# Down product of an MLP: first contributions copied by ScalarE, residual added two tiles a step later

## Chip, core and metric

One Trainium2 chip, one of its cores. The metric is the device time of one execution in microseconds (us); three executions were timed and their median is given.

## What is computed

The kernel is one layer of a streaming encoder: a mixer (gated short convolution beside a state-space scan), an output projection with a residual, then an MLP with a residual and a last normalisation. This case is about the MLP's second product:

```python
x = x + jnp.einsum("btc,cd->btd", y, w_out)                       # x1 below
h = rmsnorm(x, norm_mlp_w)
hid = jnp.square(jax.nn.relu(jnp.einsum("btd,df->btf", h, w_up)))
return x + jnp.einsum("btf,fd->btd", hid, w_down)                 # this sum, 2048 tokens x 1024
```

followed by `rmsnorm(x, final_norm_w)`. Everything is float32; 2048 tokens, width 1024, hidden width 4096.

## The kernel before

**Arithmetic.** Each operand is split into a high and a low part (`hi`, `lo`), and a product is three matmuls: hi·hi, hi·lo, lo·hi (lines 296 to 298). Matrices are multiplied in blocks of 2 x 2 by a seven-product scheme. `chain` (L265) issues the seven products of a step in the order b11, t1, t2, b21, t3, b22, t4. They run in three PSUM accumulators, called `x`, `y` and `w` (tiles `px`, `py`, `pw`): b11, t2, t3 and t4 add one after the other into `x`, t1 and b22 into `y`, b21 into `w`. ScalarE copies `x` into `w` after b11 (L303, the seed), so that b21 adds on top of b11. A product that goes on in an accumulator may start only when the value before it has been read: t3 needs the reading after t2, t4 that after t3, b22 that after t1.

**Down product.** `down` (L1036) walks `STEPS`. A step takes four hidden blocks (places) for one output block `d` of a token half `h`; near the start and the middle a step holds one or two shorter groups: step 0 is (h 0, d 0, four places), step 1 (0, 2, two places), step 2 the two groups (0, 1, one place) and (0, 3, three places), and from step 3 on four places each, with h 1 coming in at step 15. A place is 128 channels deep, so a product over four places is 12 matmuls. For each (h, d) four accumulators of 128 x 512 float32 lie in SBUF: `c11`, `c22`, `c12`, `c21` (tiles `acc`). They are made by `outs` (L1019), which at once loads the residual `x1_d` into them (L1026). `evict` (L1055) then adds each PSUM value to its accumulator on VectorE (L1069): t1 to c22, t2 to c12, b21 to c11, then t3 to c22, b22 to c12, t4 to c21. The reading after b11 is left out when the seed was made.

**Where accumulators lie.** The pool tag `utmp` has 8 tiles of 512 columns, `uhid` 5 of 2 x 512. `two` (L1029) hands them out in units; the 16 accumulators of the first half take all 8 `utmp` and four `uhid`. The fifth `uhid` is the first unit of the second half (unit 8).

**Feeding.** Weights of the next step are loaded by SyncE (`wraw`, L999), cast by ScalarE (`whi`, L100) and their low part made by VectorE (`wlo`, L101; sums of blocks L252 and L229). Hidden blocks come back from DRAM by SyncE (`rh`, L1016), are cast by ScalarE (`uh`, L368) and get their low part from VectorE (`ul`, L369). The last pair of the up product runs just before step 0, with its own evictions (L912, L915, L918, L919) and its stores (`hid_d`, L902 and L903).

**Order.** A scheduler places the instructions on each engine from the program's dependences; each engine then works through its list in that order. So the edit moves instructions beyond the lines that it touches.

Of the kernel before, what the change touches and what calls it, by code (L numbers as in the profile page):

```python
# [14 lines left out]
ALU = mybir.AluOpType  # L15
# [15 lines left out]
NBB = TH // TB  # L31
# [9 lines left out]
def trunk(ctx: ExitStack, tc: tile.TileContext, x, w_in, w_dt, w_out, w_up, w_down, cvec, hrow, out):  # L41
    nc = tc.nc
# [15 lines left out]
    x1_d = spill("x1", NB)  # L58
# [21 lines left out]
        out=tri, in_=tri, compare_op=ALU.is_ge, fill=0.0, base=0, pattern=[[1, P]], channel_multiplier=-1  # L80
# [789 lines left out]
    class Mlp(Seven):  # L870
# [148 lines left out]
        def outs(self, h, d):  # L1019

            t = {}
            self.units = 2 * d if h == 0 else max(self.units, 8)
            for two in ((("c11", 0, 0), ("c22", 4, 1)), (("c12", 0, 1), ("c21", 4, 0))):
                for a, (n, i, bb) in zip(self.two(), two):
                    t[n] = a
                    nc.sync.dma_start(a, x1_d[h * NBB + bb][:, d + i])  # L1026
            self.acc[h, d] = t

        def two(self):  # L1029
            n, self.units = self.units % 9, self.units + 1  # L1030
            if n < 4:
                return [self.tmp("acc") for _ in range(2)]
            t = self.wide("acc")
            return [t[:, i] for i in range(2)]

        def down(self, ws):  # L1036
            late = None
            for n, step in enumerate(STEPS):
                last = n + 1 == len(STEPS)
                ahead = self.rest_weights() if last else self.weights(self.load_down(STEPS[n + 1]))  # L1040
                groups = [[self.wides[h * NQ + f] for f in fs] for h, d, fs in step]
                if not last:
                    for h, d, fs in STEPS[n + 1]:
                        if (h, d) not in self.acc:
                            self.outs(h, d)
                if n == N_FIRST + 3:
                    late = self.finish_first()

                def done(name, gi):
                    h, d, fs = step[gi]  # L1050
                    if h == 0 and fs[-1] == NQ - 1:
                        i, bb = {"c11": (0, 0), "c22": (4, 1), "c12": (0, 1), "c21": (4, 0)}[name]
                        nc.sync.dma_start(fin_d[d + i][:, bb * TB : (bb + 1) * TB], self.acc[h, d][name])

                def evict(name, gi, pm):  # L1055
                    h, d, fs = step[gi]
                    c, p, fin = {
                        "b11": ("c11", "x", 0),
                        "t1": ("c22", "y", 0),
                        "t2": ("c12", "x", 0),  # L1060
                        "b21": ("c11", "w", 1),
                        "t3": ("c22", "x", 1),
                        "b22": ("c12", "y", 1),
                        "t4": ("c21", "x", 1),
                    }[name]
                    t = self.acc[h, d][c]
                    if name == "b11" and gi in self.seeds:
                        return
                    nc.vector.tensor_tensor(out=t, in0=pm[p], in1=t, op=ALU.add)  # L1069
                    if fin:  # L1070
                        done(c, gi)

                def after(name):
                    if late is not None and name in ("b11", "t2", "t3"):
                        next(late, None)
                    g = REFILL.get(n)
                    if g is not None:
                        self.refill((g,), name)
                    if last and name == "t4":
                        self.rest_blocks()  # L1080

                ws = self.chain(groups, ws, ahead, evict, after)
            for _ in late:
                pass
            self.rest(ws)
# [131 lines left out]
    for n in range(1, 2 * NQ - 3):  # L1217
        fs = list(range(n, n + 4))
        step = [(h, n % 4, [f % NQ for f in fs if f // NQ == h]) for h in range(2)]
# [228 lines left out]
    class Output:  # L1448
# [62 lines left out]
        def residual(self, n):  # L1511
            if n < len(self.UNITS):
                i, b, d = self.UNITS[n]
                t = self.xt[n] = self.xp.tile([P, TB], F32, tag="xt", name="xt", bufs=3)
                nc.sync.dma_start(t, x[b, :, d] if i == 0 else x1_d[b][:, d])
# [185 lines left out]
```

## Time and profile before

| | us |
|---|---|
| median of three executions | 2631.99 |
| lowest, highest | 2627.35, 2633.1 |
| the profiled execution's own time | 2631.43 |
| its span in the trace | 2629.4 |

The span leaves out 2.0 us of the profiled execution's own time. Matmul rows overlap: a row lasts 0.39 us, while the next one starts 0.23 us after it. A bracket such as [0.68 <-DVE acc L1069] at a row's end is the time for which the engine stood idle before it and what released it. A row "us in total, times, longest" belongs to the view of waits. In the view of windows each engine's busy time is followed by the count of its instructions; then come the granted TensorE clock, the share of the DMA engines and GB/s.

### The profile page before, as it was taken

The numbers are of one execution on the slowest core, as the hardware profiler recorded it, in microseconds if no ns is written. First come the engines' busy times: TensorE is split into PE (matmuls) and PEld (weight loads), VectorE is DVE, ScalarE is ACT, GpSimd is POOL, SyncE is SP. The second block draws the span as 40 slices with busy tenths as digits, with TensorE's granted clock in tenths as the row PEclk, the third lists the DMA queues.
The fourth block names the chain that finished last, engine by engine and source line by source line (L and its number), as shares of the span: only waits on it lengthen the run. The fifth ranks groups of instructions, "written<-read, shape, count | busy, mean of one in ns | idle before, by whom it ended". The sixth has DMA issues, their size and how long they took to land.

```text
span 2629.4 us, 33773 instructions
## 1 busy us (share of the span) xinstructions
PE 2599.6 (99%) x12139; PEld 2139.1 (81%) x12139; DVE 1917.2 (73%) x2631; ACT 1458.9 (55%) x2213; POOL 59.0 (2%) x99
## 2 busy tenths in 40 slices
PE   9999999999999999999999999999999999999998
PEld 7788888788888888878888888888887788888887
DVE  7877877777777767778677775744448877888985
ACT  7554345776667666768335555755555444444443
POOL 1010000000000000000000000000000000000001
PEclk9999999999999999999999999999999999999999
DMA  4545735555555578877656786765558544665762
GB/s 156 192 174 184 280 142 193 181 179 162 171 168 169 165 266 262 266 223 232 206 196 236 263 320 232 280 213 194 190 195 299 154 149 154 212 209 168 251 206 77
DMA packets 252167, 536.96 MB, mean 204 GB/s; under 512 B 26208, under 2 KB 93024, under 8 KB 252000
## 3 DMA queue, kind: packets, MB, share of 16 engines
q1 hardware_dynamic: 251856, 534.29, 60.7%
q8 instruction: 95, 1.56, 0.2%
q14 instruction: 72, 0.59, 0.1%
q10 hardware_dynamic: 144, 0.52, 0.1%
HBM read 354.89 MB, written 179.83 MB: 203 GB/s over the span
## 4 chain that ended last, share of the span: by engine, by line
PE 66%; issue 24%; DMA 4%; ACT 3%; DVE 2%; POOL 0%; SPq 0%; POOLq 0%; DVEq 0%; ACTq 0%
PE px L296 9%; PE px L298 9%; PE px L297 9%; PE py L296 5%; PE py L298 5%; PE py L297 5%; PE pm L113 4%; PE pm L114 4%; PE pm L115 4%; PE pw L296 2%; PE pw L298 2%; PE pw L297 2%; PE yd L1350 1%; PE yo L1347 1%; DMA dec<-rd_d 1%
## 5 line engine op out<-in xcount | busy, mean ns | idle before, releaser
L296 PE MATMUL px<-uh,whi 128*128 128x512 f32 x1672 | 656.1, 392 | 8.3 <-DVE acc L1069 5.6
L298 PE MATMUL px<-uh,wlo 128*128 128x512 f32 x1672 | 651.0, 390 | 0.0
L297 PE MATMUL px<-ul,whi 128*128 128x512 f32 x1672 | 651.0, 389 | 0.0
L296 PEld LDWEIGHTS px<-uh,whi 128*128 128x128 f32 x1672 | 313.8, 188 | 82.0 <-DVE acc L1069 4.8
L101 DVE TENSOR_TENSOR wlo<-wraw,whi 128x512 fp32r<-128x512 f32 (+1 forms) x213 | 221.4, 1039 | 212.2 <-ACT whi L100 212.1
L298 PEld LDWEIGHTS px<-uh,wlo 128*128 128x128 f32 x1672 | 313.9, 188 | 66.1 <-issue 0.2
L100 ACT CAST whi<-wraw 128x1024 fp32r<-128x1024 f32 x214 | 193.9, 906 | 310.3 <-PE px L297 217.4
L297 PEld LDWEIGHTS px<-ul,whi 128*128 128x128 f32 x1672 | 314.0, 188 | 63.6
L100 ACT CAST whi<-s 128x1024 fp32r<-128x1024 f32 x210 | 219.7, 1047 | 221.3 <-PE py L297 87.4
L296 PE MATMUL py<-uh,whi 128*128 128x512 f32 x836 | 327.3, 392 | 2.5 <-ACT eb L802 1.2
L297 PE MATMUL py<-ul,whi 128*128 128x512 f32 x836 | 325.8, 390 | 0.0
L298 PE MATMUL py<-uh,wlo 128*128 128x512 f32 x836 | 325.4, 389 | 0.0
L101 DVE TENSOR_TENSOR wlo<-s,whi 128x1024 fp32r<-128x1024 f32 x210 | 255.3, 1216 | 68.7 <-ACT whi L100 65.9
L113 PE MATMUL pm<-uh,whi 128*128 128x512 f32 (+1 forms) x648 | 251.2, 388 | 0.1
L114 PE MATMUL pm<-ul,whi 128*128 128x512 f32 (+1 forms) x648 | 247.8, 382 | 0.5 <-DVE ul L226 0.5
L115 PE MATMUL pm<-uh,wlo 128*128 128x512 f32 (+1 forms) x648 | 247.9, 383 | 0.0
L296 PEld LDWEIGHTS py<-uh,whi 128*128 128x128 f32 x836 | 156.9, 188 | 38.0 <-ACT eb L802 1.6
L298 PEld LDWEIGHTS py<-uh,wlo 128*128 128x128 f32 x836 | 157.0, 188 | 32.7
L297 PEld LDWEIGHTS py<-ul,whi 128*128 128x128 f32 x836 | 157.0, 188 | 32.1
L368 ACT CAST uh<-rh 128x1024 fp32r<-128x1024 f32 (+1 forms) x128 | 120.3, 944 | 83.0 <-PE py L298 65.7
L296 PE MATMUL pw<-uh,whi 128*128 128x512 f32 x418 | 163.3, 391 | 0.0
L298 PE MATMUL pw<-uh,wlo 128*128 128x512 f32 x418 | 162.8, 389 | 0.0
(245 smaller groups left out, 3786.6 us busy)
## 6 DMA issues: line engine op xcount, KB each, us to landing
hid_d<-e SPq DMA_DIRECT2D x96, 512.0 KB, 3.8
rh<-hid_d SPq DMA_DIRECT2D x96, 512.0 KB, 4.2
wraw<-w_in SPq DMA_DIRECT2D x68, 512.0 KB, 3.7
wraw<-w_down SPq DMA_DIRECT2D x104, 256.0 KB, 3.6
wraw<-w_up SPq DMA_DIRECT2D x48, 512.0 KB, 4.2
dec<-rd_d SPq DMA_DIRECT2D x32, 512.0 KB, 5.5
wraw<-w_out SPq DMA_DIRECT2D x32, 512.0 KB, 5.2
x_d<-xt SPq DMA_DIRECT2D x64, 256.0 KB, 3.7
```

The costliest lines, as they stand in the source:

```text
L100: nc.scalar.copy(hi, raw)
L101: eng.tensor_tensor(out=lo, in0=raw, in1=hi.bitcast(F32), op=ALU.subtract)
L113: nc.tensor.matmul(out, whi, hi, start=(k == 0), stop=False)
L114: nc.tensor.matmul(out, whi, lo, start=False, stop=False)
L115: nc.tensor.matmul(out, wlo, hi, start=False, stop=(k == nk - 1))
L296: nc.tensor.matmul(p, hi, h[0], start=not seeded and k == 0, stop=False, **kw)
L297: nc.tensor.matmul(p, hi, h[1], start=False, stop=False, **kw)
L298: nc.tensor.matmul(p, lo, h[0], start=False, stop=(k == len(g) - 1), **kw)
L368: nc.scalar.copy(p[i][0], t)
L1347: nc.tensor.matmul(yo[:, j * L : (j + 1) * L], state[:, j * P : (j + 1) * P], cT, start=True, stop=True)
L1350: nc.tensor.matmul(yd[(i % 2) * 64 : (i % 2) * 64 + 64, (i // 2) * L : (i // 2 + 1) * L], byhead(t["xdt"])[:, i, :], t["dec"][:, i % 2 * 4 ...
```

## The change

`outs` makes the accumulators of the first token half (h 0) without loading anything into them. For a step whose (h 0, d) has not been met before, the first value for each accumulator is copied there by ScalarE (`nc.scalar.copy`, L1096 after) in place of VectorE's add: after t1 (c22), t2 (c12), b21 (c11) and t4 (c21). That is four copies for each of four output blocks d, 16 in all, in steps 0, 1 and 2. The residual follows in steps 3 to 10: the new generator `residual` loads two tiles a step into one spare `uhid` tile (`res`) and adds them to their accumulators on VectorE (L1043 after), 16 loads and 16 adds. The spare tile is then handed out as unit 8, as the fifth `uhid` tile was before. The second half (h 1) is as before. The changed kernel's lines from 1024 on stand up to 30 lines further down: L1069 is L1098 there.

```diff
-            for two in ((("c11", 0, 0), ("c22", 4, 1)), (("c12", 0, 1), ("c21", 4, 0))):
+            for two in self.TWOS:
                 for a, (n, i, bb) in zip(self.two(), two):
                     t[n] = a
-                    nc.sync.dma_start(a, x1_d[h * NBB + bb][:, d + i])
+                    if h:
+                        nc.sync.dma_start(a, x1_d[h * NBB + bb][:, d + i])
             self.acc[h, d] = t
+
+        TWOS = ((("c11", 0, 0), ("c22", 4, 1)), (("c12", 0, 1), ("c21", 4, 0)))
+
+        def residual(self, m):
+
+            if self.spare is None:
+                self.spare = self.wide("res")
+            d = (m + 3) % 4
+            for j, (n, i, bb) in enumerate(self.TWOS[m // 4]):
+                nc.sync.dma_start(self.spare[:, j], x1_d[bb][:, d + i])
+            yield
+            yield
+            for j, (n, i, bb) in enumerate(self.TWOS[m // 4]):
+                t = self.acc[0, d][n]
+                nc.vector.tensor_tensor(out=t, in0=t, in1=self.spare[:, j], op=ALU.add)
+                yield
...
-            t = self.wide("acc")
+            if n == 8 and self.spare is not None:
+                t, self.spare = self.spare, None
+            else:
+                t = self.wide("acc")
...
+                left = self.residual(n - 3) if 3 <= n < 11 else iter(())
+                fresh = [h == 0 and (h, d) not in begun for h, d, _ in step]
+                begun.update((h, d) for h, d, _ in step)
...
-                    nc.vector.tensor_tensor(out=t, in0=pm[p], in1=t, op=ALU.add)
+                    if fresh[gi] and (name in ("b11", "t1", "t2", "t4") or (name == "b21" and gi in self.seeds)):
+                        nc.scalar.copy(t, pm[p])
+                    else:
+                        nc.vector.tensor_tensor(out=t, in0=pm[p], in1=t, op=ALU.add)
...
                 def after(name):
+                    next(left, None)
```

What this does to the lists of the engines, at three places. First SyncE, between the last reloads of hidden blocks for step 0 (`rh`) and the weights of step 1 (`wraw`, 128 x 256) and step 2 (`wraw`, 128 x 128 and 128 x 384); `x_d` is the residual. Before:

```order
L1016 DMA rh<-hid_d_3_116 128x512
L1026 DMA acc<-x_d_77 128x512
L902 DMA hid_d_15_144<-e_16756 128x1024
L902 DMA hid_d_15_144<-e_16757 128x1024
L1026 DMA acc<-x_d_78 128x512
L903 DMA hid_d_15_144<-t_16755 128x512
L1026 DMA acc<-x_d_78 128x512
L1026 DMA acc<-x_d_77 128x512
L999 DMA wraw<-w_down 128x256 x4
L1026 DMA acc<-x_d_77 128x512
```

And now, from the reloads of the third kind (128 x 1024) on:

```order
L999 DMA wraw<-w_down 128x256 x2
L1016 DMA rh<-hid_d_1_114 128x1024
L1016 DMA rh<-hid_d_2_115 128x1024
L1016 DMA rh<-hid_d_3_116 128x1024
L999 DMA wraw<-w_down 128x256 x2
L1016 DMA rh<-hid_d_0_113 128x512
L899 DMA b_d<-e_16756 128x512
L1016 DMA rh<-hid_d_1_114 128x512
L902 DMA hid_d_15_144<-e_16758 128x1024
L1016 DMA rh<-hid_d_2_115 128x512
L1016 DMA rh<-hid_d_3_116 128x512
L999 DMA wraw<-w_down 128x128 x2
```

The residual's loads are gone from here, and the weights of step 1 are issued ahead of seven (their first half) and of four (their second) of the reloads, where they stood behind all of them.

Second ScalarE, at the end of the same reloads (casts `uh`) and in step 1. Before:

```order
L368 CAST uh_16975<-rh 128x512
L368 CAST uh_16979<-rh 128x512
L368 CAST uh_16983<-rh 128x512
L368 CAST uh_16987<-rh 128x512
L100 CAST whi<-wraw 128x512
L100 CAST whi<-s_17071 128x512
L303 COPY pw<-px 128x512
```

Now:

```order
L368 CAST uh_16975<-rh 128x512
L100 CAST whi<-wraw 128x512
L368 CAST uh_16979<-rh 128x512
L368 CAST uh_16983<-rh 128x512
L1096 COPY acc<-py 128x512
L1096 COPY acc<-px 128x512
L1096 COPY acc<-pw 128x512
L303 COPY pw<-px 128x512
L100 CAST whi<-s_17063 128x512
L100 CAST whi<-s_17096 128x512
L100 CAST whi<-wraw 128x256
L1096 COPY acc<-px 128x512
```

The cast of step 1's first weights moved between the reloads' casts, and step 0's copies after t1, t2 and b21 stand behind the last of those casts.

Third VectorE, where the first residual adds (`res`) stand, at the turn from step 2 to step 3; two `px` adds are the readings after t3 of step 2's two groups, the `py` adds those after b22. Now:

```order
L101 TENSOR_TENSOR wlo<-s_17290,whi 128x1024
L1098 TENSOR_TENSOR acc<-px,acc 128x512 x2
L1098 TENSOR_TENSOR acc<-py,acc 128x512
L1043 TENSOR_TENSOR acc<-acc,res 128x512
L252 TENSOR_TENSOR s_17443<-wraw 128x512
L1098 TENSOR_TENSOR acc<-py,acc 128x512
L369 TENSOR_TENSOR ul_17339<-rh,uh_17338 128x1024
L101 TENSOR_TENSOR wlo<-s_17331,whi 128x1024
```

And in each of the last four of the eight steps, ahead of the readings after t1 (`py`) and t2 (`px`):

```order
L229 TENSOR_TENSOR s_17933<-wraw,s_17893 128x512
L1043 TENSOR_TENSOR acc<-acc,res 128x512 x2
L369 TENSOR_TENSOR ul_17857<-rh,uh_17856 128x1024
L1098 TENSOR_TENSOR acc<-py,acc 128x512
L1098 TENSOR_TENSOR acc<-px,acc 128x512
```

The first add stands behind step 2's readings after t3, and the later pairs behind a step's last reading and ahead of the next step's first.

TensorE's list changes too: the first product of step 1 (b11, six matmuls) moved from behind step 0's t4 to the place between step 0's b21 and b22.

```order
L298 MATMUL pw_17011<-uh1_16880,wlo_16858 128x512
L296 MATMUL px_17126<-uh0_16802,whi_17059 128x512
L297 MATMUL px_17126<-ul0_16803,whi_17059 128x512
L298 MATMUL px_17126<-uh0_16802,wlo_17060 128x512
L296 MATMUL px_17126<-uh0_16806,whi_17059 128x512
L297 MATMUL px_17126<-ul0_16807,whi_17059 128x512
L298 MATMUL px_17126<-uh0_16806,wlo_17060 128x512
L296 MATMUL py_17019<-uh2_16929,whi_16925 128x512
```

Here `px_17126` is step 1's `x`, and `pw_17011` and `py_17019` are step 0's `w` and `y`.

More of the change, by code (lines that the diff above doesn't have):

```diff
@@ L1032, in two @@
                 return [self.tmp("acc") for _ in range(2)]
-            t = self.wide("acc")
+            if n == 8 and self.spare is not None:
+                t, self.spare = self.spare, None
+            else:
+                t = self.wide("acc")
             return [t[:, i] for i in range(2)]
+        spare = None
         def down(self, ws):
             late = None
+            begun = set()
             for n, step in enumerate(STEPS):
```

## Prediction

> **What bounds the kernel now.** The page comes first: which engine fills the span.
>
> ```profile
> span 2629.4 us, 33773 instructions
> PE 2599.6 (99%) x12139; PEld 2139.1 (81%) x12139; DVE 1917.2 (73%) x2631; ACT 1458.9 (55%) x2213; POOL 59.0 (2%) x99
> ```
>
> TensorE is busy for 2599.6 of 2629.4 us, so the change can only win time in which TensorE stands still, and it removes no matmul. The second view is therefore TensorE's waits around the start of the down product (1960 to 2160 us), in total, times and longest.
>
> ```profile
> PE px L296 <- DVE acc L1069: 4.5, 3, 2.9
> PE px L296 <- DVE e L915: 0.5, 1, 0.5
> ```
>
> Most of it is TensorE waiting for VectorE's add into an accumulator, the instruction that the change takes out of steps 0 to 2. The timeline of TensorE has them one by one (one of the three is left out here); between the first wait and the next stand the first matmuls of step 0's t2 and b21.
>
> ```profile
> 1988.54 0.50 PE L296 MATMUL px<-uh,whi 128*128 128x512 f32 x1 [0.55 <-DVE e L915]
> ...
> 1993.89 0.39 PE L296 MATMUL px<-uh,whi 128*128 128x512 f32 x1
> ...
> 1996.61 0.39 PE L296 MATMUL pw<-uh,whi 128*128 128x512 f32 x1
> ...
> 2003.13 0.50 PE L296 MATMUL px<-uh,whi 128*128 128x512 f32 x1 [0.68 <-DVE acc L1069]
> ...
> 2011.89 0.50 PE L296 MATMUL py<-uh,whi 128*128 128x512 f32 x1 [0.51 <-ACT whi L100]
> ...
> 2042.65 0.47 PE L296 MATMUL px<-uh,whi 128*128 128x512 f32 x1 [2.90 <-DVE acc L1069]
> ```
>
> (The rows of 1993.89 and 1996.61 have no bracket: no wait.) Twelve matmuls went from 1993.89 to 1996.61, so one starts every 2.72 / 12 = 0.227 us. The brackets leave out what a restart costs, so I take the whole loss from the windows, which count matmuls.
>
> ```profile
> 1970.00:2000.00 30.00, 29.45 (x129) 23.80 (x128) 26.70 (x31) 23.39 (x32) 0.00 (x0) 1.00 0.91 314
> 2000.00:2030.00 30.00, 27.94 (x119) 21.61 (x118) 22.57 (x35) 9.52 (x14) 0.00 (x0) 1.00 0.90 305
> 2030.00:2060.00 30.00, 27.09 (x120) 22.10 (x119) 26.93 (x36) 12.30 (x14) 0.00 (x0) 1.00 0.56 173
> 2060.00:2090.00 30.00, 30.00 (x133) 24.62 (x132) 21.80 (x29) 11.77 (x15) 0.00 (x0) 1.00 0.52 158
> ```
>
> An undisturbed stretch holds 133 matmuls, the three before it 129, 119 and 120: 399 - 368 = 31 are missing, 31 x 0.227 = 7.0 us. That is all this change can reach. The same rows say why: up to 2030 the DMA engines are 90% busy, VectorE is at 27 of 30 us in two of the windows, and ScalarE, which the change gives the work to, at 9.5 and 12.3 of 30 after 2000.
>
> **What the change does, part by part.** I start with the readings in step 0. VectorE's rows, then ScalarE's, then SyncE's:
>
> ```profile
> 1998.64 0.68 DVE L1069 TENSOR_TENSOR acc<-py,acc 128x512 f32<-128x512 f32 x1
> 1999.24 0.68 DVE L369 TENSOR_TENSOR ul<-rh,uh 128x512 fp32r<-128x512 f32 x1
> ...
> 2002.40 0.68 DVE L1069 TENSOR_TENSOR acc<-px,acc 128x512 f32<-128x512 f32 x1
> ...
> 2040.69 1.22 DVE L369 TENSOR_TENSOR ul<-rh,uh 128x1024 fp32r<-128x1024 f32 x1
> ```
>
> ```profile
> 1975.02 0.58 ACT L912 COPY s<-py 128x512 f32<-128x512 f32 x1
> ...
> 1998.40 1.26 ACT L368 CAST uh<-rh 128x512 fp32r<-128x512 f32 x2 [1.34 <-DMA rh<-hid_d]
> 2000.53 0.62 ACT L368 CAST uh<-rh 128x512 fp32r<-128x512 f32 x1 [0.87 <-DMA rh<-hid_d]
> 2008.78 0.62 ACT L100 CAST whi<-wraw 128x512 fp32r<-128x512 f32 x1 [7.62 <-DMA wraw<-w_down]
> ```
>
> ```profile
> 1978.37 2.13 SPq L1026 DMA_DIRECT2D acc<-x_d  x4
> ...
> 2002.87 1.04 SPq L1026 DMA_DIRECT2D acc<-x_d  x2
> 2003.95 1.88 SPq L999 DMA_DIRECT2D wraw<-w_down  x4
> ```
>
> The reading after t2 starts at 2002.40, although t2 gave way to b21 at 1996.61: VectorE is 5 us behind. An add or low part of this size holds it 0.60 us (1998.64 to 1999.24). ScalarE is idle for 7.62 us from 2001.15, waiting for step 1's weights, which SyncE issued only at 2003.95, behind residual loads. So:
>
> *Step 0, b22, t3 and t4 (the two shorter of the three waits for VectorE, 4.5 - 2.9 = 1.6 us, and restarts).* VectorE loses the readings after t1 and t2; ScalarE has them at 0.58 each (the copy from PSUM to SBUF at 1975.02 is the same operation). They stand behind the last cast of the reloads. If that cast ends no earlier than before (2001.15), the copies are done at 2001.7 and 2002.3. TensorE now has six matmuls of step 1 to do first (1.36 us), and would come to b22 at about 1999.4 + 1.4 = 2000.8: a wait of 1.1 us at worst, and none if the casts come 1 us earlier, for which the four loads issued at 1978.37 (256 KB each, in a row further down) go from in front of them. t3 follows, and its reading has b22's nine remaining matmuls as cover (2.0 us against 0.68).
>
> *Step 1's weights (0.51 and a restart).* They are now issued ahead of the last reloads, over 10 us earlier by the list; the wait goes. What is late next: ScalarE's cast of step 2's weights stands ahead of the copy after step 1's t2, and a product of two places lasts only 1.4 us. One cast of 1024 columns is about 1.05 us, so t3 or t4 of step 1 may wait some 0.4 us; 0 to 0.7 as bounds (one such cast less the 0.3 us that remains of b21).
>
> *The turn to step 3 (2.90, the largest).* VectorE is late there because steps 0 to 2 piled up: at 2040.69 a low part of 1.22 us still stands in front of the reading that TensorE waits for. Of step 2's twelve readings eight go to ScalarE: 8 x 0.60 = 4.8 us off VectorE ahead of this place, more than 2.9. The first residual add stands behind the readings after t3, so it is not in their way. I take this wait as gone; its bounds are 0 and 2.90.
>
> *The first wait (0.55 at 1988.54)* hangs on the up product's reading L915, ahead of anything moved: it stays, 0.7 us with its restart.
>
> *The 16 adds in steps 3 to 10* cost VectorE 2 x 0.60 = 1.2 us a step. A step, before:
>
> ```profile
> 2081.95:2101.00 19.05, 19.05 (x86) 15.77 (x85) 14.56 (x20) 7.94 (x9) 0.00 (x0) 1.00 0.51 154
> ```
>
> ```profile
> 2085.74 1.22 DVE L369 TENSOR_TENSOR ul<-rh,uh 128x1024 fp32r<-128x1024 f32 x1 [1.13 <-ACT uh L368]
> 2086.88 0.68 DVE L1069 TENSOR_TENSOR acc<-py,acc 128x512 f32<-128x512 f32 x1
> 2089.41 0.69 DVE L1069 TENSOR_TENSOR acc<-px,acc 128x512 f32<-128x512 f32 x1 [1.85 <-PE px L298]
> ```
>
> VectorE has 19.05 - 14.56 = 4.5 us left, and 1.13 + 1.85 = 3.0 of it just where the pair of adds was put. Cost: nothing while that idle time covers it; 1.2 x 8 = 9.6 us if it were gone. The 16 loads find DMA engines at 51% in place of 90%. On SyncE a load that must wait for the add before it holds up the `rh` and `wraw` loads behind it, but those adds were done most of a step earlier.
>
> **The sum.** Against the profiled execution's own 2631.43 us (0.6 below the median): 7.0 us lost, 0.7 stays, so 6.3 us can go. New waits: 0 to 1.1 in step 0, 0 to 0.7 in step 1; 0.6 in all, nearest to the shortest wait of this kind (0.68). 2631.4 - 6.3 + 0.6 = 2625.7 us.
>
> **Rivals.** *ScalarE's list as the new queue.* Both copies of step 0, and step 1's first weights, stand behind casts that wait for reloads (1.34 and 0.87 in the rows above). If the reloads land no earlier, b11 of step 1 waits for its weights (about 1.1 us: cast at 1999.0 at the earliest, its low part 0.6 + 0.6 later, at 2000.4 where 1999.3 is wanted), and 0.7 in step 1 comes on top: 1.8 in place of 0.6, 2626.9 us; with a cast of step 2's weights in the way of one more copy (1.05), 2628.0. For it: those idle times. Against it: 1 MB less ahead of them. The Trainium skill, in "PSUM — Partial Sum Buffer", section on engine and sequencer instructions, says that the queues of ScalarE and VectorE are strictly first in, first out, which speaks against giving evictions to an engine whose casts wait for transfers. The trace agrees: the cast at 2008.78 waits 7.62 us and nothing behind it overtakes. By that rule alone 2628.0 would stand; the sum follows the row of ScalarE's load, which leaves two thirds of it free.
>
> *The turn stays late.* The `uh` and `ul` work of step 3's reloads, not the readings, sets the 2.90; then 3.1 comes back: 2628.8 us. For it: a low part, not a reading, stands right in front at 2040.69. Against it: 4.8 us less in the same list.
>
> *Slower: the adds wait for their loads.* An add on VectorE stands ahead of the readings, and if its tile has not landed, everything waits. Residual loads before took (median):
>
> ```profile
> acc<-x_d SPq DMA_DIRECT2D x18, 256.0 KB, 5.6
> ```
>
> VectorE has 4.5 - 1.2 = 3.3 us to spare in a step; a wait longer than that decides. At 5.6 us it is 2.3 us in each of eight steps, 18.4 us: 2625.7 + 18.4 = 2644 us. Against it: one spare tile is free right after a step's adds, the next pair is asked for most of a 19 us step ahead.
>
> **Chances and range.** Forecast 0.52, ScalarE's queue 0.24, late turn 0.18, slower 0.06. About 0.2%, 5.3 us, is what a measurement of this kernel can tell from no change: below 2626.7 is faster. The forecast lies there, the next two rivals lie between 2626.9 and 2628.8, within 0.2%. Faster 0.52, same 0.42, slower 0.06. Low end: all 7.0 us go, 2624.4, less the 2 us by which a median of three may lie off (they spread from 2627.35 to 2633.1): 2622.5. High end: the late turn at 2628.8 with the same 2 us, 2630.8.
>
> **What would show it.** In the changed profile, 1970 to 2060 us holds 395 matmuls or more; TensorE's wait for L1098 near 2040 is gone; the first weights of step 1 are cast before 2000; steps 3 to 10 still last 19.05 us and VectorE's adds there have no DMA as releaser. Wrong: a wait of TensorE for a ScalarE copy over 1 us in steps 0 to 2, a wait of 2 to 3 us left near 2040, or brackets naming `res` in front of VectorE's adds.

## The result and the profile after

The changed kernel takes 2626.88 us (median of 12 runs, 2621.61 to 2634.53), the kernel before 2631.54 us beside it (12 runs, 2626.45 to 2633.85). The ratio is 0.9979, 95% interval 0.997 to 0.9988: 0.21% or 5.5 us faster by the ratio, between 3 and 8 us (the medians differ by 4.7). A second measurement of the same kernel gave 0.9981 (0.9972 to 0.999). The profiled execution's own time fell from 2631.43 to 2625.58 us, so the one profile shows 5.85 us.

The page's first lines after the change: the span, and the load of each engine.

```profile
span 2623.8 us, 33814 instructions
PE 2598.3 (99%) x12139; PEld 2140.2 (82%) x12139; DVE 1916.6 (73%) x2631; ACT 1466.5 (56%) x2229; POOL 56.4 (2%) x99
```

TensorE does the same 12139 matmuls in a span that is 5.6 us shorter; what went is time in which it stood still. VectorE has as many instructions as before (16 readings went, 16 late adds came), ScalarE has 16 more.

TensorE's waits from 1960 to 2160 us, where there were 5.5 us in five waits:

```profile
PE py L296 <- ACT acc L1096: 0.3, 1, 0.3
```

And the windows of the same four stretches; behind each busy time stands the count of instructions.

```profile
1970.00:2000.00 30.00, 29.96 (x132) 24.21 (x130) 28.18 (x33) 24.52 (x35) 0.00 (x0) 1.00 0.93 315
2000.00:2030.00 30.00, 29.71 (x130) 24.30 (x131) 20.34 (x29) 17.83 (x28) 0.00 (x0) 1.00 0.65 217
2030.00:2060.00 30.00, 30.00 (x134) 24.83 (x133) 27.22 (x38) 13.89 (x17) 0.00 (x0) 1.00 0.69 213
2060.00:2090.00 30.00, 30.00 (x134) 24.84 (x133) 23.18 (x30) 12.06 (x13) 0.00 (x0) 1.00 0.55 167
```

The first three hold 132 + 130 + 134 = 396 matmuls; 28 of the 31 missing ones are back, 28 x 0.227 = 6.4 us. The DMA engines' share, the second number from the end, fell in 2000 to 2030 from 0.90 to 0.65, because the residual's loads have gone from there.

The one wait that is left is for ScalarE. TensorE's row, and ScalarE's list around it:

```profile
2000.29 0.50 PE L296 MATMUL py<-uh,whi 128*128 128x512 f32 x1 [0.33 <-ACT acc L1096]
```

```profile
1996.29 0.61 ACT L100 CAST whi<-wraw 128x512 fp32r<-128x512 f32 x1
1998.35 0.62 ACT L368 CAST uh<-rh 128x512 fp32r<-128x512 f32 x1 [1.45 <-DMA rh<-hid_d]
1999.14 0.62 ACT L368 CAST uh<-rh 128x512 fp32r<-128x512 f32 x1 [0.16 <-DMA rh<-hid_d]
1999.66 0.58 ACT L1096 COPY acc<-py 128x512 f32<-128x512 f32 x1
2000.14 0.59 ACT L1096 COPY acc<-px 128x512 f32<-128x512 f32 x1
```

The copy after t1 stands behind two casts that wait 1.45 and 0.16 us for reloads. Step 1's first weights are cast at 1996.29, where this cast stood at 2008.78. SyncE issued those weights (two and two of four loads) at:

```profile
1982.21 0.90 SPq L999 DMA_DIRECT2D wraw<-w_down  x2
...
1987.37 0.90 SPq L999 DMA_DIRECT2D wraw<-w_down  x2
```

Before, all four came at 2003.95. The late adds, as a group and the only one that waited for its load:

```profile
L1043 DVE TENSOR_TENSOR acc<-acc,res x16: 677/682/693, 2032.2 to 2154.1; 128x512 f32<-128x512 f32 x16
```

```profile
2043.05 0.69 DVE L1043 TENSOR_TENSOR acc<-acc,res 128x512 f32<-128x512 f32 x1 [0.55 <-DMA res<-x_d]
```

So the time came from the start of the down product, as forecast. What the two profiles can't say is which half of the change did it: the readings that left VectorE, or the 16 residual loads that left SyncE's list there. (Before, eight of them were issued ahead of step 1's weights and eight more ahead of step 2's.) The prediction gave the larger part (4.5 of the 5.5 us of waits) to the readings.

### The profile page after: what moved, and what is told of

The parts are those of the page before. It is cut to its first block, busy times and chain, and to the rows that moved or that the text cites. A ratio compares the mean times of both kernels' runs of the same rounds, so it can differ in the third digit from the quotient of the medians.

```text
span 2623.8 us, 33814 instructions
## 1 busy us (share of the span) xinstructions
PE 2598.3 (99%) x12139; PEld 2140.2 (82%) x12139; DVE 1916.6 (73%) x2631; ACT 1466.5 (56%) x2229; POOL 56.4 (2%) x99
## 4 chain that ended last, share of the span: by engine, by line
PE 86%; DMA 6%; DVE 4%; ACT 3%; issue 2%; SPq 0%; POOL 0%; POOLq 0%; DVEq 0%; ACTq 0%
PE px L296 13%; PE px L298 13%; PE px L297 13%; PE py L296 7%; PE py L297 7%; PE py L298 7%; PE pm L113 4%; PE pm L114 4%; PE pm L115 4%; PE pw L296 3%; PE pw L298 3%; PE pw L297 3%; PE yd L1380 1%; DMA ry<-yn_d 1%; PE yo L1377 1%
```

## The experiments

Two theories. *Readings*: VectorE was behind because it made the first contributions too; taking them off it gives the gain, and an edit that leaves VectorE as loaded gives little. *Loads*: the residual loads stood ahead of step 1's weights in SyncE's list; with the weights early, VectorE and ScalarE get their weight work done in time, and the readings matter little. The second divides again: it may be the order in the list, or the bytes.

One measure serves for all profiles: matmuls counted in the three windows from 1970 to 2060 us; (399 - count) x 0.227 is TensorE's lost time there, as in the prediction. A window's count is good to a few matmuls, since some records are missing (two profiles of the changed kernel give 396 and 400), so differences below 1 us are not read from it. The ratio is to the kernel before, from 10 to 12 executions of each edit. The profile is of one execution only: e1's was the slowest of its eleven, e2's the third slowest, e7's the second fastest. So the lost time of a row and its ratio need not agree.

| kernel | matmuls | lost, us | ratio | 95% interval |
|---|---|---|---|---|
| before, first profile | 368 | 7.0 | | |
| before, second profile | 370 | 6.6 | | |
| changed | 396 | 0.7 | 0.9979 | 0.997 to 0.9988 |
| changed, again (e0) | 400 | 0 | 0.9981 | 0.9972 to 0.999 |
| copies on VectorE (e1) | 381 | 4.1 | 0.9981 | 0.9972 to 0.999 |
| copies on VectorE, again (e12) | 386 | 3.0 | | |
| early loads kept (e2) | 377 | 5.0 | 0.9994 | 0.9982 to 1.0006 |
| late adds left out (e3) | 396 | 0.7 | 0.9979 | 0.9969 to 0.9988 |
| copy after t1 on VectorE (e4) | 389 | 2.3 | 0.9986 | 0.9975 to 0.9997 |
| early loads on GpSimd's queue (e7) | 376 | 5.2 | 1.001 | 1.0002 to 1.0019 |
| before, loads on GpSimd's queue (e8) | 348 | 11.6 | 1.0016 | 1.0006 to 1.0025 |
| before, weights first (e9) | 386 | 3.0 | 0.9982 | 0.9973 to 0.9991 |
| early loads kept, weights first (e11) | 394 | 1.1 | 0.9979 | 0.997 to 0.9988 |

A caution for all of them: a scheduler places the program anew after each edit, so an edit of one line also shifts other instructions of steps 0 to 2, on TensorE too. In the kernel before, products of steps 1 and 2 alternate there in pieces of 1 to 10 matmuls; in e9 each stands whole.

**The changed kernel once more (e0)**, to see how far one profile can be trusted.

> The changed kernel once more, beside the others, as the mark for them. Both theories: about 5 us (0.2%) faster than before, TensorE starting 6 to 7 us earlier than before once step 3 is under way.

2624.08 us beside 2630.98, and no wait of TensorE at all in 1960 to 2160. So the 0.33 us for ScalarE's copy comes and goes (it is 0.55 in e3), and the gain stands.

**The copies on VectorE (e1, and again as e12).** The loads are late as in the change, but VectorE reads everything itself:

```diff
-                        nc.scalar.copy(t, pm[p])
+                        nc.vector.tensor_copy(t, pm[p])
```

> The first contributions are copied by VectorE instead of ScalarE; the residual is still loaded and added later. Theory 1 (the gain is VectorE's relief: 16 readings of 0.6 us moved to an idle ScalarE): VectorE falls behind again, the waits for it in steps 0 and 1 (1.6 us) and at the turn to step 3 (2.9 us) come back, 4 us or more of the gain are lost. Theory 2 (the gain is that 16 loads leave SyncE's list and the DMA engines, so that reloads and weights come earlier): at most 1 us is lost.

2625.1 us, ratio 0.9981: no slower than the change. TensorE's waits of the second profile, then its row at the turn to step 3:

```profile
PE pw L296 <- ACT pw L303: 0.8, 1, 0.8
PE px L296 <- DVE acc L1096: 0.8, 1, 0.8
PE py L296 <- DVE acc L1096: 0.7, 1, 0.7
```

```profile
2038.50 0.47 PE L296 MATMUL px<-uh,whi 128*128 128x512 f32 x1 [0.75 <-DVE acc L1096]
```

The 2.90 us at the turn is 0.75 in both profiles, with VectorE as loaded as before. Both lose 3 to 4 us where the change loses under 1; 0.7 to 0.8 of it is a wait for ScalarE's seed copy (L303), which is not a reading of VectorE. The timed runs don't show those 2 to 3 us; their interval is 2.4 us to each side.

> The changed kernel with the copies on VectorE once more, for a second profile, since the first showed half of the stage's gain lost while its times did not. If the waits of 1.47 and 0.75 us for VectorE's copies are its own, they are there again (some 2 us in all, 3.3 us gained up to step 5); if they were scatter, one or both are gone and the gain is 5 to 7 us.

The wait at the turn (0.75) and that for the seed copy (0.66 in e1, 0.77 here) came again. The 1.47 us in step 1 did not; 0.71 us in step 0 stands in its place. So some 2 us of small waits are the kernel's own.

**The early loads kept (e2).** The copies are ScalarE's; the residual loads stay where they were, without use, since the copies overwrite them:

```diff
-                    if h:
-                        nc.sync.dma_start(a, x1_d[h * NBB + bb][:, d + i])
+                    nc.sync.dma_start(a, x1_d[h * NBB + bb][:, d + i])
```

> The changed kernel, but the residual is also loaded into the accumulators at once as before; the copies overwrite it, so these 16 loads are useless and only put the traffic and SyncE's order of before back. Theory 1 (VectorE's relief): at most 1.5 us of the gain is lost, no wait of 2 to 3 us near the turn to step 3. Theory 2 (the loads): the weights of step 1 are cast after 2008 again, 3 to 5 us of the gain are lost.

2627.1 us, ratio 0.9994 (0.9982 to 1.0006): not to be told from the kernel before. The executions are uneven: eight of the eleven lie from 2624.88 to 2628.32, three from 2630.87 to 2637.53, and the profile is of one of the three. So the interval does not exclude most of the change's gain either. SyncE, ScalarE, TensorE, each with the rows of step 1's first weights:

```profile
1998.62 2.24 SPq L1026 DMA_DIRECT2D acc<-x_d  x3
2000.90 1.85 SPq L999 DMA_DIRECT2D wraw<-w_down  x4
```

```profile
2006.78 0.62 ACT L100 CAST whi<-wraw 128x512 fp32r<-128x512 f32 x1 [1.51 <-DMA wraw<-w_down]
```

```profile
2007.45 0.50 PE L296 MATMUL px<-uh,whi 128*128 128x512 f32 x1 [2.81 <-ACT whi L100]
```

The waits for VectorE's readings are gone, the turn's 2.90 too, and TensorE, now earlier, waits 2.81 us for weights that stand behind the residual loads as before. A wait has taken the place of the one removed, and TensorE's clock fell behind it, which cost another 1.7 us (last section). In this profile, taking the readings off VectorE is not enough; the times alone don't prove it.

**The late adds left out (e3).** The first token half gets no residual; nothing is loaded or added in steps 3 to 10:

```diff
-                left = self.residual(n - 3) if 3 <= n < 11 else iter(())
+                left = iter(())
```

> The changed kernel without the residual of the first token half: its 16 late loads and 16 late adds are left out (that half of the sum lacks x1). Both theories: VectorE has room for the adds in steps 3 to 10, so the time is within 1 us of the changed kernel. The rival that the late adds cost something: 2 us or more faster than the changed kernel.

2623.84 us beside 2630.98, ratio 0.9979: 16 loads and 16 adds cost nothing that can be measured.

**The kernel before, weights first (e9).** Nothing of the change but the order in SyncE's list: `outs` for the next step is called after t4 in place of the step's start. Same bytes, same adds on VectorE.

```diff
-                if not last:
-                    for h, d, fs in STEPS[n + 1]:
-                        if (h, d) not in self.acc:
-                            self.outs(h, d)
...
+                    if name == "t4" and not last:
+                        for h, d, fs in STEPS[n + 1]:
+                            if (h, d) not in self.acc:
+                                self.outs(h, d)
```

> The kernel before, with one edit: the loads for the next step's accumulators are asked for after t4 in place of the step's start, so that step 1's weights stand ahead of most residual loads in SyncE's list; the same bytes and the same adds. If the order in SyncE's list is the cause, the wait for step 1's weights (0.51) goes and the time falls by 2 to 4 us (2627 to 2629), unless VectorE's first adds of step 1 now wait for residual tiles that land late, which would show as waits of VectorE for x_d and eat the gain. If VectorE's readings are the cause, 2631 us and the 2.9 at the turn to step 3 stays.

2626.08 us beside 2630.66, ratio 0.9982 (0.9973 to 0.9991): the change's gain, without the change. SyncE's list, in which step 1's weights (L999) now stand ahead of all but the first four residual loads (L1026), then the cast (step 2's weights follow at 2002.31, ahead of the last eight):

```profile
1994.49 0.42 SPq L999 DMA_DIRECT2D wraw<-w_down  x1
...
1995.68 0.43 SPq L999 DMA_DIRECT2D wraw<-w_down  x1
...
1999.45 0.92 SPq L999 DMA_DIRECT2D wraw<-w_down  x2
2000.41 1.86 SPq L1026 DMA_DIRECT2D acc<-x_d  x4
```

```profile
1999.60 0.62 ACT L100 CAST whi<-wraw 128x512 fp32r<-128x512 f32 x1 [1.88 <-DMA wraw<-w_down]
```

This execution runs 3.0 us ahead (its first four residual loads are issued at 1975.37, where before they were at 1978.37), so 1999.60 answers to 2002.6 before, 6.2 us sooner than 2008.78. TensorE's waits, and the turn's row:

```profile
PE px L296 <- DVE acc L1065: 1.8, 2, 1.1
```

```profile
2035.37 0.47 PE L296 MATMUL px<-uh,whi 128*128 128x512 f32 x1 [1.09 <-DVE acc L1065]
```

The wait for weights is gone, and the turn's 2.90 is 1.09 with not one reading taken off VectorE. No accumulator waited for its residual. The DMA share from 2000 to 2030 stayed at 0.92: the bytes do no harm behind the weights.

**Weights first and ScalarE's copies (e11).** e2 with e9's reordering: the useless loads are still made.

> The changed kernel with the early residual loads kept, without use (the copies overwrite them), and with step 1's weights asked for ahead of them, as in the run that only reorders the loads; the late loads and adds stay. It adds to that order what ScalarE's copies bring. If the order in SyncE's list is the main term and VectorE's relief a second, smaller one, TensorE has no wait for VectorE in 1960 to 2160 us (the order alone left 0.68 and 1.09), its gain up to step 5 is 6 to 7 us in place of 4.5, and the time is 2624 to 2626 us, not to be told from the order alone by the times. If the early bytes cost time wherever they stand, it is 2627 us or more, with a wait for weights.

2623.61 us beside 2628.67, ratio 0.9979. One wait is left:

```profile
PE px L296 <- DVE acc L1093: 0.2, 1, 0.2
```

The edits of e2 and e11 differ only in where the same loads stand: 5.0 against 1.1 us lost, ratio 0.9994 against 0.9979, intervals that just overlap. e9 and e11 differ in who reads (and in the late adds): 3.0 against 1.1 us lost, which the times, 0.9982 and 0.9979, can't tell apart.

**The loads on another queue (e7, e8).** e7 is e2 with the useless loads issued by GpSimd, so that SyncE's list is the changed kernel's; e8 is the kernel before with the same edit:

```diff
-                    nc.sync.dma_start(a, x1_d[h * NBB + bb][:, d + i])
+                    (nc.sync if h else nc.gpsimd).dma_start(a, x1_d[h * NBB + bb][:, d + i])
```

> The changed kernel, with the early residual loads kept, without use (the copies overwrite them), and issued by GpSimd's queue: the bytes of before are moved, SyncE's list is that of the changed kernel. If the 18 loads cost time by standing ahead of step 1's weights in SyncE's list, this is as fast as the changed kernel (2624 to 2626 us beside 2631 of before) and step 1's first weights are cast before 2000. If their bytes cost time, by keeping the DMA engines busy where the reloads and weights land, it is as the kernel with early loads on SyncE (2627 to 2629) and TensorE again waits 2 to 3 us for step 1's weights. If VectorE's relief were all that counts, it is as fast as the changed kernel too.

> The kernel before, with one edit: the early residual loads of the first token half are issued by GpSimd's queue in place of SyncE's; all readings stay VectorE's adds. If VectorE's readings set the loss, nothing changes (2631 us, waits for VectorE of 1.6 us in step 0 and 2.9 at the turn to step 3). If the place in SyncE's list does, most of the gain comes without the change (2626 to 2628 us; the wait for step 1's weights gone, the turn to step 3 under 1 us). If the bytes do, 2630 to 2632 with the wait for the weights still there.

Both are slower than the kernel before: 2632.49 and 2633.78 us beside 2630.66. So it is not SyncE's own time that counts. The DMA view of e7 from 1996 to 2020 us, the median from issue to landing at the end:

```profile
acc<-x_d POOLq DMA_DIRECT2D x8, 256.0 KB, 6.9
...
wraw<-w_down SPq DMA_DIRECT2D x4, 192.0 KB, 7.5
```

The same view of the changed kernel:

```profile
wraw<-w_down SPq DMA_DIRECT2D x4, 192.0 KB, 3.0
```

On another queue the residual goes beside the weights: step 2's weights take 7.5 in place of 3.0 us. The Trainium skill's "DMA: Bandwidth & Descriptors", section "Issuing engines are not separate DMA queues", says that transfers started by different engines run on the same 16 DMA engines and interleave; these two rows agree. VectorE's row in e7, then TensorE's:

```profile
2013.86 0.69 DVE L252 TENSOR_TENSOR s<-wraw 128x512 f32<-128x512 f32 x1 [5.91 <-DMA wraw<-w_down]
```

```profile
2019.62 0.50 PE L296 MATMUL px<-uh,whi 128*128 128x512 f32 x1 [1.79 <-DVE acc L1097]
```

VectorE stands 5.91 us with nothing that may overtake, and its readings are late for that. In e8 the same wait is 5.4 us and TensorE's 4.86. The wait is booked on an accumulator of VectorE; the cause is a transfer.

That is a third of e7's 5.2 us. The larger part lies ahead of it: a wait of 1.84 us at 1988.58 for L915's reading, which is 2.11 in e8 and at most 0.55 in every profile without loads on GpSimd's queue. In e7 it stands behind low parts of VectorE that waited 1.01 and 0.52 us for casts, and these casts had waited 1.18 and 0.69 us for reloads; GpSimd issued its first residual loads shortly before, from 1963 to 1977. TensorE's clock fell behind this wait, which cost another 1.7 us (last section).

**The copy after t1 on VectorE (e4)**, against ScalarE's list as the last wait of the change:

```diff
-                        nc.scalar.copy(t, pm[p])
+                        (nc.vector.tensor_copy if name == "t1" and n == 0 else nc.scalar.copy)(t, pm[p])
```

> The changed kernel, with step 0's reading after t1 copied by VectorE in place of ScalarE; one of the two copies that stand behind ScalarE's last cast of the reloads goes. If ScalarE's list is what costs the 0.33 us at 2000.29 in the changed profile, that wait goes and the time is the changed kernel's or up to 0.5 us below (2624 to 2626), too little to be told by the times; if VectorE is the tighter one there, a wait for VectorE of 0.5 to 0.7 us appears in its place.

The 0.33 us is gone and 0.7 us for VectorE's copy stands in its place; 2628.17 us, ratio 0.9986 (0.9975 to 0.9997), no better. Nothing here speaks for VectorE as the reader.

**The kernel before once more (e10)**, one execution.

> The kernel before once more, for a second profile. If the waits of the first one are the kernel's own, the wait for step 1's weights (0.5 us) and the one at the turn to step 3 (2 to 3 us) are there again. The first wait, 0.55 us at L915's reading, came and went among runs that don't touch it, so it may be absent; then its loss is scatter and not a term of this change.

The wait at L915's reading is absent. The other four are there again; 0.54 and 0.87 for VectorE in step 0 (0.68 and 0.88 before), and three of the four rows are:

```profile
2006.57 0.47 PE L296 MATMUL px<-uh,whi 128*128 128x512 f32 x1 [0.87 <-DVE acc L1069]
...
2011.85 0.50 PE L296 MATMUL py<-uh,whi 128*128 128x512 f32 x1 [0.51 <-ACT whi L100]
...
2042.59 0.47 PE L296 MATMUL px<-uh,whi 128*128 128x512 f32 x1 [2.90 <-DVE acc L1069]
```

0.51 and 2.90 came again to the hundredth, and the loss is 6.6 in place of 7.0 us, too close to say what the first wait costs.

## Why the prediction was right, and where its reasons were not

The forecast was 5.7 us less than before; measured are 5.5 by the ratio and 5.85 in the profile. The place of the gain was right. That the size came out as well is in part luck: terms that the sum had wrong went against each other (the first wait went, later waits came), and the change does two things at once, so it didn't matter for its time which of them the sum put the gain down to.

- *7.0 us are all that can be reached.* Right: the change loses 0.7 and 0 us there in two profiles.
- *Step 0: a new wait of 0 to 1.1 us behind ScalarE's casts.* Right, at the low end: 0.33 us once, none in the second profile, 0.55 in e3. (By the prediction's own times the upper bound is 2001.7 - 2000.8 = 0.9 us; in the same way its rival for b11 comes to 1999.0 + 1.2 = 2000.2, not 2000.4. Nothing hangs on either.)
- *Step 1's weights: 0.51 us and a restart go.* The wait went for the reason given, but the term was mis-sized. The prediction read the weights' lateness only from the wait that TensorE shows for it. It reached much further: the order of the loads alone (e9) brings the lost time from 7.0 to 3.0 us, 4 us in place of 0.7, and in the times all that can be measured. While the weights are out, ScalarE's casts and VectorE's sums and low parts of them are put off, and then stand in front of the readings. Before, VectorE stood still for step 1's weights, and came late to the first sum of step 2's, whose lateness the prediction left out:

```profile
2009.43 0.69 DVE L101 TENSOR_TENSOR wlo<-wraw,whi 128x512 fp32r<-128x512 f32 x1 [2.54 <-ACT whi L100]
...
2021.44 0.68 DVE L252 TENSOR_TENSOR s<-wraw 128x512 f32<-128x512 f32 x1
```

In e9 the first has no wait, and the second starts here, about 6 us sooner once its 3.0 us of lead are taken off:

```profile
2012.35 0.68 DVE L252 TENSOR_TENSOR s<-wraw 128x512 f32<-128x512 f32 x1
```

- *The turn to step 3: 2.90 us go because eight readings leave VectorE.* The wait went, and it is gone in e2 too, where at least part of that is the readings' doing (TensorE's pause of 2.81 us ahead of it also gives VectorE time). But the reason was not needed: with all readings on VectorE, early weights bring it to 1.09 (e9) or, with the loads out of the way, 0.75 (e1, e12). The count of eight is off too. The reading that TensorE waited for came after step 2's t4:

```profile
2041.83 0.68 DVE L1069 TENSOR_TENSOR acc<-px,acc 128x512 f32<-128x512 f32 x1
```

It is itself one of the eight, and the other reading after t4 stands behind it. So six stood ahead, 3.6 us in place of 4.8, which is still more than 2.9.
- *What carried the gain.* The prediction booked 4.5 of 5.5 us of waits as VectorE's readings, since they are what the waits name. The profiles don't bear that out. Early weights add 18 matmuls where VectorE reads (368 to 386, e9) and 17 where ScalarE does (377 in e2 to 394 in e11), some 4 us each time; ScalarE's copies add 9 (368 to 377, e2) and 8 (386 in e9 to 394 in e11), some 2 us. (Against e1 and e12 the change is 2.3 to 3.4 us better, 0.7 to 0.8 of it the wait for the seed copy.) The times show the order's gain clear of noise (e9). They don't show one of the readings: not alone (e2, whose interval is wide), and not on top of the order (e11 beside e9). Which of the two is larger is not shown: e2's count holds the 1.7 us of the clock's fall, and without it the copies alone would have won nearly as much as the order. What is shown is that the order alone is enough.
- *The first wait stays, 0.7 us.* Wrong: it is absent in the change and in the second profile of before. It comes and goes in the same kernel, and what it costs is too little for the counts.
- *The 16 late adds cost nothing.* Right (e3). One did wait for its load, 0.55 us; the prediction had none, and had named a bracket with `res` in front of VectorE's adds as a sign of being wrong. No wait of TensorE stands behind it.
- *Later waits.* Not foreseen: from 2160 to 2600 us TensorE's waits for residual and accumulator adds sum to 2.2 us where they were 1.2.

```profile
PE px L296 <- DVE acc L1098: 1.3, 3, 0.6
PE px L296 <- DVE res L1098: 0.9, 1, 0.9
```

They lie behind the last add (2154.1); with the same late adds e11 shows 0.5 us there, and e3, without them, 1.5. So nothing ties them to the adds, and why they vary stays open. They take back part of the 6.4 us won; the whole profile shows 5.85.

Of the rivals, ScalarE's list as the new queue did not come about: the price was 0 to 0.33 us in the changed kernel, not 1.8. Nor did the late turn, or the adds that wait for their loads beyond VectorE's spare time. The Trainium skill's "PSUM — Partial Sum Buffer", section "Engine vs sequencer instructions", has the queues of ScalarE and VectorE as strictly first in, first out; the traces agree at each place above (the copy at 1999.66 behind two waiting casts, VectorE's 5.91 us in e7 with its readings behind it), but the rule says nothing of how long the first in line waits, and that was what decided.

What stays open: whether the order of TensorE's own products, which the scheduler changed along with the loads, has a share in e9's gain; and whether VectorE's relief is worth anything in the times. On the first, two things are on record. In e8 the products of steps 1 and 2 stand whole as in e9, and it loses 11.6 us, so that order alone does not bring the gain. But where VectorE reads everything, the wait at the turn is 0.75 to 1.09 us in each profile with whole products (e1, e12, e8, e9) and 2.90 in the two with pieces (before, e10), so the pieces may have a part in the 2.90.

No version tried beats the changed kernel by more than the measurements can tell; e9 and e1 can't be told from it.

## What to carry to other kernels

A wait that names a reading may be a late transfer two engines upstream: look at what the list of the engine that reads did in the 10 to 30 us before, and at what DMA it or its feeder stood still for. Before moving work between engines, try the order of the loads: putting what is needed first at the front of the one queue gave, in the times, all of the gain here. A second queue was no way out here, with the DMA engines 95% and 81% busy (e7, the first two windows): the loads went beside the urgent ones and made them late.

## What the hardware showed that was not expected

After a pause TensorE's granted clock can fall to half for some 3 us. Windows of e2 around its pause of 2.81 us (the clock is the third number from the end):

```profile
2007.40:2009.00 1.60, 1.55 (x5) 0.98 (x6) 1.57 (x4) 0.00 (x1) 0.00 (x0) 0.87 0.92 330
2009.00:2011.00 2.00, 2.00 (x6) 1.13 (x5) 1.74 (x4) 1.83 (x4) 0.00 (x0) 0.50 0.92 236
2011.00:2013.00 2.00, 2.00 (x8) 1.60 (x7) 0.44 (x2) 0.58 (x2) 0.00 (x0) 0.75 1.04 351
2013.00:2015.00 2.00, 2.00 (x10) 1.68 (x9) 0.00 (x0) 0.69 (x2) 0.00 (x0) 1.00 0.78 266
```

By the clocks that is 0.13 x 1.6 + 0.50 x 2 + 0.25 x 2 = 1.7 us lost on top of the pause; at half speed, 1.7 us are lost in 3.4. The pause's length alone does not decide. In e7 the clock fell after a wait of 1.84 us (0.53 in the 2 us that follow this row, 1.7 us lost again):

```profile
1988.50:1990.50 2.00, 1.93 (x5) 1.58 (x6) 2.00 (x4) 2.00 (x5) 0.00 (x0) 0.61 0.88 244
```

In the kernel before it did not after 2.90 us:

```profile
2042.60:2044.60 2.00, 1.95 (x9) 1.63 (x10) 2.00 (x3) 0.00 (x0) 0.00 (x0) 1.00 0.84 197
```

The Trainium skill's "TensorE: Matmul & The Clock Gate", section on the HAM clock gate, tells of such a fall to half after an idle window of about 3.4 us, in windows that run free of the program. The halving agrees with 0.50, and free-running windows would let equal pauses end differently; but a fall after 1.84 us of waiting is earlier than an idle window of 3.4 us allows. So part of what e2 and e7 lose is this clock and not the wait itself, and a short wait is not always as cheap as its bracket.
